# Attention scores by two heads and transposes by block, with projection matmuls between the pieces

## The chip, the cores and the metric

One core of one Trainium2 chip runs the whole program. The metric is the device time of one execution in microseconds (us), lower is better. Engines are called PE (matrix multiplication), DVE (vector), ACT (activation functions and copies), POOL (general) and SP (which issues most transfers).

## The reference

A two-layer encoder over two requests that share weights, 512 and 256 tokens of width 1024, all in 32-bit floats. Each layer is a half SwiGLU block, a mixer, and another half SwiGLU block; a final RMSNorm ends it. The first layer's mixer, the only part that the change touches, is this:

```python
def mixer_ab(h, w_in, sgu_ln_g, sgu_ln_b, sgu_w, sgu_b, sink, w_out):
    z = h @ w_in
    zs = gelu(z[..., :1024])
    u, vh = zs[..., :512], layer_norm(zs[..., 512:], sgu_ln_g, sgu_ln_b)
    vh = vh.reshape(B, L // 128, 128, 4, 128)
    vmix = einsum('gij,bnjgc->bnigc', sgu_w, vh) + sgu_b
    a_out = u * vmix                                      # gating half
    q, k, v = the other columns of z: 8 q heads, 2 k heads, 2 v heads of 64
    b_out = window_gqa(rope_partial(q), rope_partial(k), v, sink)
    return concatenate([a_out, b_out], axis=-1) @ w_out
```

`window_gqa` works on blocks of 128 queries. Each block sees the keys of its own block and of its two neighbours within 128 positions, four q heads share one k and v head, and one learned number per head (`sink`) joins the softmax as an extra column without a value.

## The kernel before, in words

Activations are kept transposed, features on the 128 partitions and tokens along the free axis, so 768 columns in all. A matmul of 32-bit floats is made of three products of rounded parts: each operand is split in a high part (ACT copies it to a rounded type) and a low part (DVE subtracts the high part from the original), and PE computes high times high, high times low and low times high into one PSUM bank. `mm3` issues these three, called a triple here. Weights arrive by transfer as `raw` and are split into `whi` (ACT) and `wlo` (DVE).

PE executes in the order in which the code is written. The order of the other engines' instructions is set by a scheduler from its own model. The written order is woven from a main line and side chains. The main line of the first mixer projects the q heads (`q_heads`, m = 0 to 3), the gating input (`vh_part`, called for three token blocks at a time: three PSUM tiles of 512 columns), the gate (`u_part`), and then the output (`mixer_out`). A side chain is a Python generator. It issues some work and yields a number, the microseconds of modelled PE work that must be issued before it goes on. After every triple `mm3` calls `tick()`, which resumes the chains whose number is due. `drain` runs a chain to its end at once, without triples between.

Three kinds of side chain matter here. `attention(GAP0)` walks over 12 steps, kv = 0, 1 and n = 0 to 5. A step has three parts. `score` issues the score matmuls of four q heads in two pairs m = 0, 1 (`scores2`, six matmuls a pair), and then the softmax in `finish_rows`: a DVE reduce for each head that adds the mask and finds the maximum, a negation, an ACT exponential for each head with its sum, the sink's exponential, a sum, a reciprocal and a DVE multiply for each head. `turn` transposes the probabilities, four PE transposes for each of two or three key blocks into one PSUM bank, and splits each bank into `th` (ACT) and `tl` (DVE). `values` multiplies with the values, copies half of the bank with ACT (`tb`) and adds the halves with four DVE instructions (`o`). The values of a step come after the scores of the next. The chains `sgu` (one for each of six token blocks) normalise a block of the gating input (`vg`), split it (`vhh`, `vhl`), mix it on PE with `mixed` (12 small matmuls) and scale and shift it from PSUM with four DVE instructions, also named `o`, at L1319. The third kind, `v_tokens`, prepares the values early.

PSUM has eight banks. The pool `mm` has four, used in turn by the projections, and `aux` has four, used in turn by scores, transposes, values and gating. A bank is taken again only when the engine that reads it has done so. The q heads' projections are read by `roped` on DVE: a shuffle (`ru`), two multiplications (`rt`, `ru`) and an add.

At the start of the output projection, `mixer_out` begins two output tiles with the inputs whose split is `e` (`eh`, `el`), and then goes on with inputs whose split is made there (`oh`, `ol`), by `parts`:

```python
            with self.tc.high_priority(), self.tc.issue_after(self.exps[-1]):
                parts(rest, 0)
```

`self.exps` is a list to which `finish_rows` appends its last exponential each time it is called, so that these splits come on ACT after the latest one written so far. What remains of the attention chain is drained near the end of that function.

Of the kernel before, what the change touches and what calls it, by code (L numbers as in the profile page):

```python
# [9 lines left out]
F32 = mybir.dt.float32  # L10
# [6 lines left out]
P = 128  # L17
# [29 lines left out]

WTOTAL = 12 * D * FF + 16 * EARLY * P * D + D * 1792 + 2 * D * D + D * 3072 + D * 512
VTOK = (4.0,9.0)
GAP0 = 5.2  # L50
SGU = (8.0, 3.0, 4.0)
NP, NQ = 16, 2
GAPS1 = (3.5, 0.6, 3.5, 0.8)
# [2 lines left out]
class Trunk:  # L56
# [1061 lines left out]
    def mixer0(self):  # L1118
        nc = self.nc
        mp = self.mixer_open("m0")  # L1120
# [8 lines left out]
        msk = mp.tile([P, 3 * P], F32, tag="msk", name="msk")  # L1129
        nc.sync.dma_start(msk, self.aps["gmask"])  # L1130
        sink = mp.tile([P, P], F32, tag="sink", name="sink")[:, :8]
# [18 lines left out]
        def roped(ps, c0, c1):  # L1150
            n = c1 - c0
            t, u = tmp("rt")[:, :n], tmp("ru")[:, :n]
            nc.vector.stream_shuffle(out=u, in_=ps[:, :n], mask=swap)
            nc.vector.tensor_tensor(out=t, in0=ps[:, :n], in1=rct[:, c0:c1], op=ALU.mult)
            nc.vector.tensor_tensor(out=u, in0=u, in1=rst[:, c0:c1], op=ALU.mult)
            nc.vector.tensor_tensor(out=t, in0=t, in1=u, op=ALU.add)
            return t
# [18 lines left out]
        for g in (0, 1):  # L1176
            c0, c1 = GROUPS[g]
            t = roped(pkv[g][0], c0, c1)
# [17 lines left out]
                self.q_split(*qs[g], t)  # L1196
            qheads.append(qs)

        def score(kv, qs, n):
            lo_b, hi_b = (0, 4) if n < 4 else (4, 6)  # L1200
            blks = list(range(max(n - 1, lo_b), min(n + 2, hi_b)))
            nk = len(blks)
            cols = slice(blks[0] * P, (blks[-1] + 1) * P)
            ps_list, ps = [], None
            for m in (0, 1):
                if nk == 3 or m == 0:
                    ps = [self.psum(self.aux, "aux") for _ in (0, 1)]
                o = 0 if nk == 3 else m * nk * P
                dst = [t[:, o : o + nk * P] for t in ps]
                q = [t[:, n % 4 * P : (n % 4 + 1) * P] for t in qs[m][n // 4]]  # L1210
                self.scores2(dst, q, (kh[kv][:, cols], kl[kv][:, cols]))
                ps_list += dst
            p = [mp.tile([P, 3 * P], F32, tag="p", name="p", bufs=4) for _ in range(4)]
            m0 = (blks[0] - n + 1) * P
            add = msk[:, m0 : m0 + nk * P]
            outs = [p[r][:, : nk * P] for r in range(4)]
            self.finish_rows(
                mp, 4, ps_list, outs, [add] * 4,
                [sink[:, 4 * kv + r : 4 * kv + r + 1] for r in range(4)], sink[:, 4 * kv : 4 * kv + 4],
            )  # L1220
            return kv, n, blks, p

        def turn(kv, n, blks, p):
            res = []
            for i, b in enumerate(blks):
                pt = self.psum(self.aux, "aux")
                for r in range(4):
                    self.tpose(pt[:, r * P : (r + 1) * P], p[r][:, i * P : (i + 1) * P])
                th = mp.tile([P, 512], F32R, tag="th", name="th", bufs=3)
                tl = mp.tile([P, 512], F32R, tag="tl", name="tl", bufs=3)  # L1230
                self.split(th, tl, pt)
                res.append((th, tl))
            return res

        def values(kv, n, blks, tt):
            po = self.psum(self.aux, "aux")
# [15 lines left out]
        qheads, scored, gates = [], [], []  # L1252
# [3 lines left out]
        def attention(gap):  # L1256
            cur = None
            for kv in (0, 1):
                for n in range(6):
                    while len(qheads) < 2 * kv + 2:  # L1260
                        yield 0.5
                    new = score(kv, qheads[2 * kv : 2 * kv + 2], n)
                    scored.append((kv, n))
                    yield gap
                    if cur:
                        values(*cur[:3], tt)
                        valued.append(cur[:2])
                    yield gap
                    cur = new
                    tt = turn(*cur)  # L1270
                    yield 0.3 * gap
            yield 1.0
            values(*cur[:3], tt)

# [10 lines left out]
        def offsets():  # L1285

            b = vhl()
            self.split(*b, lnb)
            yield VTOK[0]
            ps = self.psum(self.aux, "aux")  # L1290
            mixed(ps, b)
            nc.vector.tensor_tensor(out=sb, in0=ps, in1=sb, op=ALU.add)
# [65 lines left out]

        self.spawn(offsets())
        att = self.spawn(attention(GAP0))  # L1360
        for m in range(2):
            q_heads(m)
# [457 lines left out]
```

## Time and profile before

| | us |
|---|---|
| median of 3 runs | 2595.67 |
| lowest and highest | 2592.29, 2597.21 |
| profiled execution | 2597.41 |
| its span in the profile | 2595.6 |
| PE busy | 2556.4 (98%) |
| DVE busy | 2232.9 (86%) |
| ACT busy | 1365.6 (53%) |
| POOL busy | 159.7 (6%) |
| mean granted clock of PE | 0.994 of full speed |

The span is the time from the first to the last instruction in the profile; 1.8 us of the execution lie around it. An engine's busy time is the sum of its instructions. The granted clock is what a throttle leaves of PE's full speed: 0.5 means that matmuls take twice as long. The first mixer takes about 545 to 745 us of the span. Line numbers such as L1248 are those of the kernel before; in the changed kernel they are shifted by one or two.

### The profile page before, as it was taken

What the parts mean: (1) busy time and instruction counts of PE and PEld (TensorE: products, weight loads), DVE (VectorE), ACT (ScalarE), POOL (GpSimd) and SP (SyncE); (2) the same over time, 40 slices, a digit from 0 to 9 for tenths busy, and PEclk for the clock granted to TensorE, in tenths of its full rate; (3) what the DMA queues carried; (4) which work ended last, traced back from release to release, by engine and by line L of the source; (5) the groups of instructions that cost most, each with busy time, mean ns of one, the idle gap of its engine ahead of it and who ended that gap; (6) DMA issues with size and microseconds to landing.
All of it is one profiled execution on the core that took longest, in us unless ns stands there. A gap on an engine that the chain in (4) does not pass through costs nothing.

```text
span 2595.6 us, 41312 instructions
## 1 busy us (share of the span) xinstructions
PE 2556.4 (98%) x15114; PEld 2491.2 (96%) x15114; DVE 2232.9 (86%) x4659; ACT 1365.6 (53%) x2869; POOL 159.7 (6%) x255
## 2 busy tenths in 40 slices
PE   8999999999999999999999999999999999999998
PEld 8899999988899999999999999998998999999997
DVE  7898889888789998889998888986676699888897
ACT  7454454556656544445655445454454565444543
POOL 1000000000022000000100000002222220000000
PEclk9999999999999999999999999999999999999999
DMA  7523222321135322223442222142221344222222
GB/s 253 160 84 111 66 74 74 130 93 45 49 111 165 103 66 66 77 70 98 125 120 74 73 66 82 66 142 66 64 64 41 106 130 123 82 71 77 70 68 75
DMA packets 93372, 238.68 MB, mean 92 GB/s; under 512 B 21488, under 2 KB 34288, under 8 KB 93168
## 3 DMA queue, kind: packets, MB, share of 16 engines
q1 hardware_dynamic: 85712, 218.96, 26.5%
q0 software_dynamic: 7168, 16.78, 3.0%
q8 instruction: 119, 1.95, 0.3%
q14 instruction: 85, 0.70, 0.1%
q10 hardware_dynamic: 288, 0.29, 0.0%
HBM read 226.56 MB, written 15.07 MB: 93 GB/s over the span
## 4 chain that ended last, share of the span: by engine, by line
PE 68%; DVE 4%; ACT 1%; issue 1%; DMA 0%; DVEq 0%; ACTq 0%
PE ps_mm L152 41%; PE ps_aux L152 25%; PE ps_aux L156 1%; DVE wlo L123 0%; DVE tmp L415 0%; ACT p L1103 0%; DVE p L1113 0%; DVE p L1097 0%; DMA raw<-in_w 0%; ACT whi L122 0%; DVE tl L209 0%; DVE qk L1577 0%; DVE sg L589 0%; ACT diag L306 0%; DVE v L588 0%
## 5 line engine op out<-in xcount | busy, mean ns | idle before, releaser
L122 ACT CAST whi<-s 128x512 fp32r<-128x512 f32 x496 | 304.6, 620 | 404.5 <-DVE s L737 179.2
L122 ACT CAST whi<-raw 128x512 fp32r<-128x512 f32 x504 | 306.1, 619 | 224.3 <-PE ps_mm L152 95.3
L123 DVE TENSOR_TENSOR wlo<-s,whi 128x512 fp32r<-128x512 f32 x496 | 336.6, 684 | 59.9 <-ACT whi L122 50.4
L123 DVE TENSOR_TENSOR wlo<-raw,whi 128x512 fp32r<-128x512 f32 x468 | 319.9, 692 | 17.4 <-ACT whi L122 14.2
L152 PE MATMUL ps_aux<-dt,whi 128*128 128x384 f32 x864 | 221.8, 337 | 5.1 <-ACT whi L122 5.1
L152 PE MATMUL ps_mm<-db,whi 128*128 128x384 f32 x864 | 219.3, 334 | 0.0
L152 PEld LDWEIGHTS ps_aux<-dt,whi 128*128 128x128 f32 x864 | 157.7, 190 | 5.8 <-ACT whi L122 5.8
L152 PEld LDWEIGHTS ps_mm<-db,whi 128*128 128x128 f32 x864 | 156.0, 188 | 0.0
L152 PE MATMUL ps_aux<-dt,wlo 128*128 128x384 f32 x432 | 145.7, 337 | 0.2 <-DVE wlo L123 0.2
L152 PE MATMUL ps_mm<-xh,whi 128*128 128x512 f32 (+1 forms) x416 | 145.7, 350 | 0.0
L152 PE MATMUL ps_mm<-db,wlo 128*128 128x384 f32 x432 | 144.3, 334 | 0.0
L152 PE MATMUL ps_mm<-xh,wlo 128*128 128x512 f32 (+1 forms) x416 | 140.8, 338 | 0.0
L152 PE MATMUL ps_mm<-xl,whi 128*128 128x512 f32 (+1 forms) x416 | 140.8, 338 | 0.0
L737 DVE TENSOR_TENSOR s<-raw,raw 128x512 f32<-128x512 f32 x124 | 83.9, 685 | 25.1 <-DMA raw<-in_w 25.0
L577 DVE TENSOR_TENSOR u<-ps_aux,u 128x384 f32<-128x384 f32 x176 | 96.9, 551 | 7.6 <-PE ps_aux L152 7.4
L793 DVE TENSOR_TENSOR x<-ps_aux,x 128x384 f32<-128x384 f32 x160 | 85.3, 551 | 15.6 <-PE ps_aux L152 15.6
L152 PE MATMUL ps_aux<-dh,whi 128*128 128x384 f32 x384 | 97.5, 334 | 0.0
L123 POOL TENSOR_TENSOR wlo<-raw,whi 128x512 fp32r<-128x512 f32 x36 | 48.5, 1355 | 746.0 <-ACT whi L122 738.1
L1103 ACT ACTIVATE p<-p,st 128x256 f32<-128x256 f32 (+3 forms) x144 | 69.0, 480 | 47.9 <-DVE st L1101 47.8
L793 DVE TENSOR_TENSOR x<-ps_mm,x 128x384 f32<-128x384 f32 x160 | 85.8, 550 | 5.8 <-PE ps_mm L152 5.5
L572 ACT COPY u<-ps_mm 128x384 f32<-128x384 f32 x176 | 83.4, 474 | 10.7 <-PE ps_mm L152 10.4
L152 PEld LDWEIGHTS ps_mm<-xh,whi 128*128 128x128 f32 x416 | 79.2, 190 | 9.1 <-issue 0.8
(516 smaller groups left out, 8143.1 us busy)
## 6 DMA issues: line engine op xcount, KB each, us to landing
raw<-in_w SPq DMA_DIRECT2D x346, 512.0 KB, 3.7
s<-in_w POOLq DMA_DIRECT2D x64, 256.0 KB, 4.9
xdm<-x SPq DMA_DIRECT2D x16, 384.0 KB, 2.4
x<-in_x SPq DMA_DIRECT2D x16, 192.0 KB, 5.4
tok<-in_xt SPq DMA_DIRECT2D x12, 256.0 KB, 6.9
xold<-xdm SPq DMA_DIRECT2D x8, 384.0 KB, 3.1
x<-xdm SPq DMA_DIRECT2D x8, 384.0 KB, 4.5
out_y<-y SPq DMA_DIRECT2D x8, 384.0 KB, 2.6
```

Source lines behind the costliest of these rows:

```text
L122: nc.scalar.copy(hi, src)
L123: (eng or nc.gpsimd).tensor_tensor(out=lo, in0=src, in1=hi.bitcast(F32), op=ALU.subtract)
L152: self.nc.tensor.matmul(out, lhsT=lhsT, rhs=rhs, start=start, stop=stop, **kw)
L156: self.nc.tensor.transpose(out, src, self.ident)
L572: nc.scalar.copy(e[n, out], bank[key, n])
L577: nc.vector.tensor_tensor(out=t, in0=bank[key, n], in1=t, op=ALU.add)
L737: f = lambda o, x, y, op: self.nc.vector.tensor_tensor(out=o, in0=x, in1=y, op=op)
L793: nc.vector.tensor_tensor(out=o, in0=ps, in1=o, op=ALU.add)
L1103: ins = nc.scalar.activation(outs[i], outs[i], AF.Exp, bias=nm[:, i : i + 1], accum_out=sm[:, i : i + 1])
```

## The change

`score` becomes a generator that works on two heads at a time. Each pair takes two PSUM banks of its own (before, steps with two key blocks put both pairs into the same two banks), runs its six score matmuls, calls `finish_rows` for its two heads, and yields 1.5. `turn` becomes a generator that yields 0.8 after each block's four transposes. `attention` waits 3.4 (before 5.2) between the parts, and the pause of 0.3 times the gap after `turn` goes.

```diff
@@ -47,7 +47,8 @@
 
 WTOTAL = 12 * D * FF + 16 * EARLY * P * D + D * 1792 + 2 * D * D + D * 3072 + D * 512
 VTOK = (4.0,9.0)
-GAP0 = 5.2
+GAP0 = 3.4
+FINE = 1.5, 0.8
 SGU = (8.0, 3.0, 4.0)
 NP, NQ = 16, 2
 GAPS1 = (3.5, 0.6, 3.5, 0.8)
@@ -1196,32 +1197,29 @@
                 self.q_split(*qs[g], t)
             qheads.append(qs)
 
-        def score(kv, qs, n):
+        def score(kv, qs, n, res):
             lo_b, hi_b = (0, 4) if n < 4 else (4, 6)
             blks = list(range(max(n - 1, lo_b), min(n + 2, hi_b)))
             nk = len(blks)
             cols = slice(blks[0] * P, (blks[-1] + 1) * P)
-            ps_list, ps = [], None
+            m0 = (blks[0] - n + 1) * P
+            add = msk[:, m0 : m0 + nk * P]
+            p = []
             for m in (0, 1):
-                if nk == 3 or m == 0:
-                    ps = [self.psum(self.aux, "aux") for _ in (0, 1)]
-                o = 0 if nk == 3 else m * nk * P
-                dst = [t[:, o : o + nk * P] for t in ps]
+                dst = [self.psum(self.aux, "aux")[:, : nk * P] for _ in (0, 1)]
                 q = [t[:, n % 4 * P : (n % 4 + 1) * P] for t in qs[m][n // 4]]
                 self.scores2(dst, q, (kh[kv][:, cols], kl[kv][:, cols]))
-                ps_list += dst
-            p = [mp.tile([P, 3 * P], F32, tag="p", name="p", bufs=4) for _ in range(4)]
-            m0 = (blks[0] - n + 1) * P
-            add = msk[:, m0 : m0 + nk * P]
-            outs = [p[r][:, : nk * P] for r in range(4)]
-            self.finish_rows(
-                mp, 4, ps_list, outs, [add] * 4,
-                [sink[:, 4 * kv + r : 4 * kv + r + 1] for r in range(4)], sink[:, 4 * kv : 4 * kv + 4],
-            )
-            return kv, n, blks, p
-
-        def turn(kv, n, blks, p):
-            res = []
+                two = [mp.tile([P, 3 * P], F32, tag="p", name="p", bufs=4) for _ in range(2)]
+                heads = slice(4 * kv + 2 * m, 4 * kv + 2 * m + 2)
+                self.finish_rows(
+                    mp, 2, dst, [t[:, : nk * P] for t in two], [add] * 2,
+                    [sink[:, 4 * kv + 2 * m + r : 4 * kv + 2 * m + r + 1] for r in range(2)], sink[:, heads],
+                )
+                p += two
+                yield FINE[0]
+            res.append((kv, n, blks, p))
+
+        def turn(res, kv, n, blks, p):
             for i, b in enumerate(blks):
                 pt = self.psum(self.aux, "aux")
                 for r in range(4):
@@ -1230,7 +1228,7 @@
                 tl = mp.tile([P, 512], F32R, tag="tl", name="tl", bufs=3)
                 self.split(th, tl, pt)
                 res.append((th, tl))
-            return res
+                yield FINE[1]
 
         def values(kv, n, blks, tt):
             po = self.psum(self.aux, "aux")
@@ -1259,16 +1257,16 @@
                 for n in range(6):
                     while len(qheads) < 2 * kv + 2:
                         yield 0.5
-                    new = score(kv, qheads[2 * kv : 2 * kv + 2], n)
+                    new = []
+                    yield from score(kv, qheads[2 * kv : 2 * kv + 2], n, new)
                     scored.append((kv, n))
                     yield gap
                     if cur:
                         values(*cur[:3], tt)
                         valued.append(cur[:2])
                     yield gap
-                    cur = new
-                    tt = turn(*cur)
-                    yield 0.3 * gap
+                    cur, tt = new[0], []
+                    yield from turn(tt, *cur)
             yield 1.0
             values(*cur[:3], tt)
```

In the rows below, a row is one instruction with its line, its kind, what it writes and reads, and the shape; "x4" stands for so many alike in a row, and a number behind a name tells one tile from another.

The first place is PE at the third q heads' projection (`ps_mm_6380` and `ps_mm_6456`, 512 and 256 columns). Before, transposes of one step (kv 0, n 1) and scores of the next come as blocks:

```order
L152 MATMUL ps_mm_6380<-xh_5309,wlo_6373 128x512
L156 MATMUL ps_aux_6419<-ident,p 128x128 x4
L156 MATMUL ps_aux_6428<-ident,p 128x128 x4
L156 MATMUL ps_aux_6437<-ident,p 128x128 x4
L152 MATMUL ps_mm_6456<-xh_5302,whi_6372 128x256
L152 MATMUL ps_mm_6456<-xl_5310,whi_6372 128x256
L152 MATMUL ps_mm_6456<-xh_5302,wlo_6373 128x256
L152 MATMUL ps_aux_6460<-kh_5716,q_6008 128x384
L152 MATMUL ps_aux_6461<-kh_5716,q_6008 128x384
```

The changed kernel there (the same projection is `ps_mm_6394` and `ps_mm_6461`):

```order
L157 MATMUL ps_aux_6430<-ident,p 128x128 x4
L153 MATMUL ps_mm_6394<-xh_5309,whi_6390 128x512
L153 MATMUL ps_mm_6394<-xl_5317,whi_6390 128x512
L153 MATMUL ps_mm_6394<-xh_5309,wlo_6391 128x512
L157 MATMUL ps_aux_6442<-ident,p 128x128 x4
L153 MATMUL ps_mm_6461<-xh_5302,whi_6386 128x256
L153 MATMUL ps_mm_6461<-xl_5310,whi_6386 128x256
L153 MATMUL ps_mm_6461<-xh_5302,wlo_6387 128x256
L153 MATMUL ps_mm_6461<-xh_5303,whi_6386 128x256
L153 MATMUL ps_mm_6461<-xl_5311,whi_6386 128x256
L153 MATMUL ps_mm_6461<-xh_5303,wlo_6387 128x256
L157 MATMUL ps_aux_6468<-ident,p 128x128 x4
```

One or two triples now stand between blocks of four transposes, and the second score piece of the step moves to the end of this projection, right ahead of the next one's start, `vh_part(3)`:

```order
L153 MATMUL ps_aux_6516<-kh_5716,q_6094 128x384
L153 MATMUL ps_mm_6461<-xh_5308,whi_6390 128x256
L153 MATMUL ps_mm_6461<-xl_5316,whi_6390 128x256
L153 MATMUL ps_mm_6461<-xh_5308,wlo_6391 128x256
L153 MATMUL ps_mm_6461<-xh_5309,whi_6390 128x256
L153 MATMUL ps_mm_6461<-xl_5317,whi_6390 128x256
L153 MATMUL ps_mm_6461<-xh_5309,wlo_6391 128x256
L153 MATMUL ps_mm_6557<-whi_6562,xh_5302 128x512
L153 MATMUL ps_mm_6557<-wlo_6563,xh_5302 128x512
```

Those scores (`ps_aux_6516` is the last of them) are now followed on PE by two triples of 256 columns and then by the three tiles of `vh_part(3)` (`ps_mm_6557`, 6558, 6559).

DVE at the same place, before (6380 is the PSUM tile of the third q heads):

```order
L1097 ISA p,st<-ps_aux_6469,msk,sink 128x384
L1097 ISA st 128x1
L209 TENSOR_TENSOR vhl<-vg,vhh 128x512
L1101 TENSOR_SCALAR st<-st 128x4
L209 TENSOR_TENSOR vhl<-vg,vhh 128x512
L1107 TENSOR_TENSOR st<-sink,st 128x4
L123 TENSOR_TENSOR wlo_6609<-raw_6602,whi_6608 128x512
L1248 TENSOR_TENSOR o_5934<-ps_aux_6384,tb 64x128 x2
L1248 TENSOR_TENSOR o_5935<-ps_aux_6384,tb 64x128 x2
L1153 STREAM_SHUFFLE ru<-ps_mm_6380 128x512
L1154 TENSOR_TENSOR rt<-ps_mm_6380,rct 128x512
```

And DVE in the changed kernel (the same tile is 6394):

```order
L1098 ISA p,st<-ps_aux_6515,msk,sink 128x384
L1108 TENSOR_TENSOR st<-sink,st 128x2
L1246 TENSOR_TENSOR o_5934<-ps_aux_6407,tb 64x128 x2
L1246 TENSOR_TENSOR o_5935<-ps_aux_6407,tb 64x128 x2
L1098 ISA p,st<-ps_aux_6516,msk,sink 128x384
L1098 ISA st 128x1
L1154 STREAM_SHUFFLE ru<-ps_mm_6394 128x512
L1102 TENSOR_SCALAR st<-st 128x2
L210 TENSOR_TENSOR vhl<-vg,vhh 128x512
L1156 TENSOR_TENSOR ru<-ru,rst 128x512
L1155 TENSOR_TENSOR rt<-ps_mm_6394,rct 128x512
```

The last read of the tile, `rt`, still comes behind the scores' reduces, but those belong to matmuls that now stand later on PE, and one `vhl` and `ru` have moved ahead of it.

The second place is ACT at the start of the output projection (`oh_7589` and its like are the splits made by `parts`), before:

```order
L1103 ACT_TABLE_LOAD
L1103 ACTIVATE p,st<-p,st 128x384 x4
L1108 ACTIVATE st<-st 128x4
L208 CAST oh_7589<-o_5930 128x384
L208 CAST oh_7590<-o_5931 128x384
L208 CAST oh_7591<-o_5932 128x384
```

The changed kernel there:

```order
L1349 ACTIVATE ug<-ug 128x256
L1104 ACT_TABLE_LOAD
L1104 ACTIVATE p,st<-p,st 128x384 x2
L1109 ACTIVATE st<-st 128x2
L1104 ACTIVATE p,st<-p,st 128x384 x2
L1109 ACTIVATE st<-st 128x2
L209 CAST oh_7618<-o_5930 128x384
L209 CAST oh_7619<-o_5931 128x384
```

The exponentials ahead of the casts are of the same step (kv 1, n 2) but come in pairs, each with its sink's, and a gate tile (`ug`) has moved ahead of them. On PE the last score piece whose exponentials stand there (`ps_aux_7658`) now comes two triples ahead of the first that reads `oh`; before, some 50 rows lay between. The changed kernel's PE:

```order
L153 MATMUL ps_aux_7658<-kh_5717,q_6962 128x384
L153 MATMUL ps_mm_7679<-eh_5938,whi_7638 128x384
L153 MATMUL ps_mm_7679<-el_5940,whi_7638 128x384
L153 MATMUL ps_mm_7679<-eh_5938,wlo_7639 128x384
L153 MATMUL ps_mm_7679<-eh_5939,whi_7638 128x384
L153 MATMUL ps_mm_7679<-el_5941,whi_7638 128x384
L153 MATMUL ps_mm_7679<-eh_5939,wlo_7639 128x384
L153 MATMUL ps_mm_7650<-oh_7618,whi_7642 128x384
```

## The prediction

> **What bounds the kernel now.** First the totals of the page and its chain of waits, to see which engine sets the end.
>
> ```profile
> span 2595.6 us, 41312 instructions
> PE 2556.4 (98%) x15114; PEld 2491.2 (96%) x15114; DVE 2232.9 (86%) x4659; ACT 1365.6 (53%) x2869; POOL 159.7 (6%) x255
> PE 68%; DVE 4%; ACT 1%; issue 1%; DMA 0%; DVEq 0%; ACTq 0%
> ```
>
> PE is busy 98% of the span and is most of the chain. The matmuls are the same before and after, so the change can only give or take PE's idle time and the clock at which PE runs, and only in the first mixer, 545 to 745 us. Next the table of stretches there (columns: us, then busy time with count for PE, PE's weight loads, DVE, ACT and POOL, then the granted clock, DMA share and GB/s).
>
> ```profile
> 570.00:597.00 27.00, 24.25 (x136) 20.01 (x135) 23.69 (x78) 20.50 (x43) 0.00 (x0) 1.00 0.14 40
> 597.00:607.00 10.00, 9.48 (x49) 7.87 (x50) 8.39 (x26) 1.84 (x4) 0.00 (x0) 0.66 0.16 52
> 632.00:642.00 10.00, 8.54 (x45) 6.76 (x44) 9.93 (x32) 3.89 (x11) 0.00 (x0) 0.83 0.09 26
> 660.00:700.00 40.00, 37.98 (x231) 32.53 (x229) 33.34 (x85) 31.29 (x67) 4.66 (x3) 1.00 0.10 31
> 700.00:710.00 10.00, 8.10 (x41) 7.43 (x41) 7.45 (x18) 1.90 (x4) 1.29 (x1) 0.83 0.40 137
> sum 215.00, PE 206.13 PEld 181.28 DVE 172.66 ACT 124.62 POOL 16.43; mean PE 22.90 PEld 20.14 DVE 19.18 ACT 13.85 POOL 1.83
> ```
>
> The sum is over nine stretches, 545 to 760, of which these five lose most: PE idles 215 − 206.13 = 8.9 us. The clock column costs more: three stretches of 10 us at 0.66, 0.83 and 0.83, that is 10 × (0.34 + 0.17 + 0.17) = 6.8 us. So 15.7 us, 0.6% of the time, is the most that the change can gain. Who PE waited for is in its waits from 545 to 745 (idle us, count, longest).
>
> ```profile
> PE ps_aux L152 <- DVE tl L209: 3.4, 5, 1.5
> PE ps_mm L152 <- DVE wlo L123: 1.9, 1, 1.9
> PE ps_aux L156 <- DVE o L1319: 1.7, 1, 1.7
> PE ps_mm L152 <- DVE ol L209: 0.8, 1, 0.8
> ```
>
> All of these are waits for DVE: a backlog, not latency alone. In the timeline the longest three stand at the start of, or inside, the three stretches with the lower clock (start us, duration, engine, in brackets the wait before):
>
> ```profile
> 596.94 0.66 PE L156 MATMUL ps_aux<-ident,p 128*128 128x128 f32 x4 [1.66 <-DVE o L1319]
> 635.48 0.33 PE L152 MATMUL ps_aux<-swh,vhh 128*128 128x128 f32 x1 [1.46 <-DVE tl L209]
> 705.45 0.44 PE L152 MATMUL ps_mm<-oh,wlo 128*128 128x384 f32 x1 [1.90 <-DVE wlo L123]
> ```
>
> **The change, part by part.** Durations come from the groups by line and shape from 545 to 745 (busy us, mean ns).
>
> ```profile
> L1097 DVE CUSTOM_DVE_ANT_0 p<-ps_aux,msk,sink 128x384 f32<-128x384 f32 x16 | 9.0, 612 | 0.2 <-PE ps_aux L152 0.2
> L209 DVE TENSOR_TENSOR tl<-ps_aux,th 128x512 fp32r<-128x512 f32 x28 | 18.1, 683 | 6.2 <-ACT th L208 6.1
> L209 DVE TENSOR_TENSOR vhl<-vg,vhh 128x512 fp32r<-128x512 f32 x6 | 4.0, 688 | 1.8 <-ACT vhh L208 1.8
> L1248 DVE TENSOR_TENSOR o<-ps_aux,tb 64x128 f32<-64x128 f32 x48 | 16.2, 337 | 1.9 <-ACT tb L1242 1.3
> L1153 DVE STREAM_SHUFFLE ru<-ps_mm 128x512 f32<-128x512 f32 x3 | 2.2, 743 | 0.1
> L1154 DVE TENSOR_TENSOR rt<-ps_mm,rct 128x512 f32<-128x512 f32 x3 | 2.0, 674 | 0.0
> L1155 DVE TENSOR_TENSOR ru<-ru,rst 128x512 f32<-128x512 f32 x3 | 2.0, 682 | 0.0
> L1101 DVE TENSOR_SCALAR st<-st 128x4 f32<-128x4 f32 x12 | 2.0, 163 | 0.1
> L209 DVE TENSOR_TENSOR ol<-o,oh 128x384 fp32r<-128x384 f32 x16 | 8.3, 551 | 0.1
> L1103 ACT ACTIVATE p<-p,st 128x384 f32<-128x384 f32 x16 | 9.7, 604 | 3.9 <-DVE st L1101 3.9
> L1103 ACT ACT_TABLE_LOAD x7 | 9.0, 1283 | 0.1
> L208 ACT CAST th<-ps_aux 128x512 fp32r<-128x512 f32 x28 | 15.0, 589 | 19.3 <-PE ps_aux L156 19.2
> L208 ACT CAST oh<-o 128x384 fp32r<-128x384 f32 x16 | 7.4, 519 | 3.4 <-DVE o L1248 3.4
> L1108 ACT ACTIVATE st<-st 128x4 f32<-128x4 f32 x12 | 2.3, 188 | 0.0
> ```
>
> And what a projection triple (three matmuls) takes, from the first and the ninth matmul in a row of 512 columns in the timeline (start us, duration, the rest): 1.83 us for eight, 0.229 each, so 0.69 for a triple of 512, 0.52 for 384, 0.34 for 256.
>
> ```profile
> 545.03 0.39 PE L152 MATMUL ps_mm<-xh,whi 128*128 128x512 f32 x1
> 546.86 0.39 PE L152 MATMUL ps_mm<-xh,wlo 128*128 128x512 f32 x1
> ```
>
> *Removed.* Scores no longer come in twelves, nor transposes in eights and twelves, so the waits above lose their place: I count all 8.9 us as gone and price what stands in the new order as new waits. That includes the 1.9 us for wlo: in the new DVE order the subtraction of that weight stands ahead of the probability multiplies.
>
> *Added.* Four small DVE instructions (maximum negated, sink add, sum add, reciprocal) now run twice for each of 12 steps: 48 × 0.163 = 7.8 us, and 12 more exponentials of 0.188 on ACT, which two fewer table loads pay. DVE is free for 42 us of the 215, so the 7.8 us are hidden except where it is full (9.93 of 10 in the stretch from 632); if that cover went everywhere they would cost 7.8. I put them at 0 and let the waits below carry them. POOL's and SP's orders do not change, so no DMA is issued elsewhere.
>
> *New wait 1, start of the second gating projection.* Three 512-column tiles take new banks of the four in the pool mm. The third must wait until DVE has read the rotary product of the third q heads. After the second score piece, PE has two triples of 256 and two of 512: 2.1 us. On DVE ahead of that read now stand a reduce, a sink add, four o, the other reduce, the shuffle, a negation, a vhl, ru and rt: 0.61 + 0.16 + 1.35 + 0.61 + 0.74 + 0.16 + 0.69 + 0.68 + 0.67 = 5.7 us. Wait 5.7 − 2.1 = 3.6. Lower end 2.0, if the first reduce, the o and the adds run while PE still scores (1.35 + 0.16 off); upper end 5.5, if the transposes just ahead also queue for the gating groups' DVE work as they did for 1.7. I take 3.5, nearest the plain sum. Before, that read came here, and no wait for it is in PE's list:
>
> ```profile
> 589.32 0.67 DVE L1154 TENSOR_TENSOR rt<-ps_mm,rct 128x512 f32<-128x512 f32 x1
> ```
>
> *New wait 2, start of the output projection.* Its first o splits are issued only after the last exponential that has been issued by then (the list `exps`). Before, this was the sink exponential of a step whose scores lay well ahead:
>
> ```profile
> 682.99 0.19 ACT L1108 ACTIVATE st<-st 128x4 f32<-128x4 f32 x1
> 683.08 1.32 ACT L208 CAST oh<-o 128x384 fp32r<-128x384 f32 x3
> 687.46 0.33 PE L152 MATMUL ps_mm<-oh,whi 128*128 128x384 f32 x1
> ```
>
> The cast was done over 3 us before PE came to it. Now the last exponential belongs to a score piece that stands two e triples, 1.03 us, ahead of the first o triple on PE. Behind it come two reduces, a negation, two exponentials, the sink's, an oh and an ol: 1.22 + 0.16 + 1.21 + 0.19 + 0.52 + 0.55 = 3.85, less 1.03: lower end 2.8. Upper end 6.2: ACT must also do a table load and the first pair's exponentials first, 1.28 + 1.21 + 0.19, and another 0.7 is one DVE instruction such as tl in front. I take 5.0, above the middle, because DVE has ol, o, wlo and the multiplies of the first pair waiting there, and is busy 33.34 of 40 us in that stretch.
>
> *New wait 3, second group of the gating mix.* A score piece waits for a tl that stands behind two vhl, shuffle, rt and ru: 1.38 + 0.74 + 1.36 = 3.5, and 4.2 with the final rotary add, which no row above shows apart and which I estimate at rt's 0.67. PE has some 2.5 us there (seven 256 triples 2.4). I take 1.6; ends 0 and 5.3 (4.2 with another 1.1 of gating work ahead).
>
> *New wait 4, the end of attention.* Eight transposes and four value matmuls come without a triple between: th 0.59 and tl 0.68, 1.27 in all, little of it covered. 1.2, ends 0 and 1.5.
>
> *What stays of the old waits* where DVE is full: 1.0, ends 0 (the pieces are spread enough) and 3.5 (the tl waits just as now).
>
> *Clock.* New waits 1, 2 and 3 are as long as those with which the three half-clock stretches began, so I expect about three again: 0, ends −5.1 (only one short stretch stays, 6.8 − 1.7) and +3.4 (two more of 1.7).
>
> [...]
>
> *Sum.* −8.9 + 3.5 + 5.0 + 1.6 + 1.2 + 1.0 + 0 = +3.4 us. The profiled execution took 2597.41, 1.74 above the median of 2595.67; so 2600.8 in its frame, 2599.1 in the median's.
>
> **The rivals.** *Slower, by the output projection.* New wait 2 comes to its upper end, 6.2, since nothing can pass the last exponential on ACT, wait 1 to 4.5, and each pulls one more half-clock stretch of 1.7: −8.9 + 4.5 + 6.2 + 3.8 + 3.4 = +9.0, 2604.7. It decides where wait 2 passes 5.1 with those two stretches left in place: −8.9 + 4.5 + 5.1 + 3.8 = 4.5, and any clock loss then takes it over 5.2. For it: DVE's load and an ACT queue in order. Against it: ACT is only 58% busy here (124.62 of 215), so the first pair may be done early.
>
> *Faster, the pieces do their work.* Waits 1 and 2 at their lower ends (2.0, 2.8), 0.8 for wait 3, 0.9 for the rest, and all but one short half-clock stretch gone: −8.9 + 6.5 − 5.1 = −7.5, 2588.2. For it: every wait of before was one for DVE behind a burst, and DVE has 42 us free. Against it: the two dependences of waits 1 and 2 are fixed by the order, whatever the pieces.
>
> *The transposes themselves pull the clock down*, and blocks of four with a triple between no longer do. Then the three stretches go and the waits stay as forecast: +3.4 − 6.8 = −3.4, 2592.3. Against it: this row, twelve in a row at full clock (the stretch from 660 has 1.00).
>
> ```profile
> 689.02 1.47 PE L156 MATMUL ps_aux<-ident,p 128*128 128x128 f32 x12
> ```
>
> [...]
>
> **How the numbers follow.** 0.2%, 5.2 us, is about what a measurement of this kernel can tell from no change: faster is under 2590.5, slower over 2600.9. The forecast has 0.43, of which 0.07 lies over 2600.9 (its own range is 2594 to 2603); the slower rival 0.25; the faster one 0.25; the transposes' 0.07, of which 0.02 under 2590.5. So faster 0.27, same 0.41, slower 0.32. The range goes from 2588, which leaves out half of the faster rival (0.12), to 2607, which leaves out a third of the slower one (0.08).
>
> **What would show it.** In the waits of the changed kernel: a ps_mm wait for DVE rt of 2 to 5 us at the start of the second gating projection (about 588 us); a ps_mm wait for oh or ol of 3 to 6 us at the first o triple (about 685 us); wlo gone from the list. In the stretches: three at less than full clock. Wrong it would be if both waits are under 2 us, because DVE or ACT takes the pieces in another order of time than I read, or if the clock stays at 1.00 after waits of 3 us, or if half speed follows each piece.

## The result and the profile after

The changed kernel took 2600.73 us (median of 13 runs, 2598.01 to 2607.46), the kernel before on the same chips 2594.58 (13 runs, 2591.77 to 2598.29). The ratio is 1.0025, with a 95% interval from 1.0018 to 1.0032: slower by about 6 us. The profiled execution took 2600.43, with a span of 2598.7.

The totals of the changed kernel's page:

```profile
span 2598.7 us, 41352 instructions
PE 2557.5 (98%) x15114; PEld 2487.8 (96%) x15114; DVE 2237.6 (86%) x4707; ACT 1365.8 (53%) x2879; POOL 158.5 (6%) x255
```

PE has the same 15,114 matmuls, and DVE the 48 more instructions. PE's waits in the first mixer, 540 to 760 us (idle us, count, longest), stand against the list of before:

```profile
PE ps_mm L153 <- ACT oh L209: 4.2, 1, 4.2
PE ps_mm L153 <- DVE rt L1155: 3.0, 1, 3.0
PE ps_aux L153 <- DVE tl L210: 2.3, 3, 1.1
PE ps_aux L153 <- ACT th L209: 0.9, 1, 0.9
PE ps_mm L153 <- DVE ol L210: 0.6, 1, 0.6
PE ps_aux L153 <- DVE vhl L210: 0.2, 1, 0.2
```

Of the waits of before, those for wlo and both o are gone, and tl has shrunk. (The second wait for an o, the smaller one, was this row in the kernel before.)

```profile
PE ps_aux L152 <- DVE o L1248: 0.5, 1, 0.5
```

In their place stand one for oh, at the first o triple, and one for rt, at the third tile of `vh_part(3)`. In the timeline:

```profile
584.40 0.39 PE L153 MATMUL ps_mm<-xh,whi 128*128 128x256 f32 x1
589.00 0.69 DVE L1155 TENSOR_TENSOR rt<-ps_mm,rct 128x512 f32<-128x512 f32 x1
589.74 0.50 PE L153 MATMUL ps_mm<-whi,xh 128*128 128x512 f32 x1 [2.97 <-DVE rt L1155]
633.87 0.33 PE L153 MATMUL ps_aux<-swh,vhh 128*128 128x128 f32 x1 [0.58 <-DVE tl L210]
686.18 2.15 ACT L209 CAST oh<-o 128x384 fp32r<-128x384 f32 x5
686.73 0.45 PE L153 MATMUL ps_mm<-oh,whi 128*128 128x384 f32 x1 [4.19 <-ACT oh L209]
737.73 1.58 DVE L1246 TENSOR_TENSOR o<-ps_aux,tb 64x128 f32<-64x128 f32 x4
738.88 0.49 PE L153 MATMUL ps_aux<-th,vt 128*128 128x512 f32 x1 [0.86 <-ACT th L209]
740.51 0.50 PE L153 MATMUL ps_aux<-tl,vt 128*128 128x512 f32 x1 [1.13 <-DVE tl L210]
```

Stretches of the changed kernel, 545 to 765 us (busy us and count of PE, PE's weight loads, DVE, ACT, POOL, then PE's granted clock, DMA share, GB/s), and the same sum of the kernel before behind them:

```profile
545.00:600.00 55.00, 51.42 (x284) 41.89 (x283) 46.19 (x147) 32.11 (x69) 0.00 (x0) 0.97 0.19 59
600.00:645.00 45.00, 44.19 (x261) 36.00 (x261) 37.89 (x135) 27.76 (x63) 0.00 (x0) 1.00 0.17 58
645.00:685.00 40.00, 37.53 (x231) 31.33 (x230) 34.65 (x101) 29.43 (x64) 3.87 (x3) 1.00 0.16 47
685.00:700.00 15.00, 12.64 (x66) 11.94 (x66) 10.26 (x26) 5.68 (x15) 0.93 (x1) 0.89 0.08 26
700.00:730.00 30.00, 30.00 (x186) 27.21 (x185) 23.01 (x70) 12.56 (x34) 4.27 (x4) 1.00 0.31 97
730.00:765.00 35.00, 33.01 (x181) 31.78 (x178) 24.69 (x63) 16.61 (x37) 6.39 (x5) 0.95 0.33 110
sum 220.00, PE 208.79 PEld 180.14 DVE 176.68 ACT 124.16 POOL 15.46; mean PE 34.80 PEld 30.02 DVE 29.45 ACT 20.69 POOL 2.58
```

```profile
sum 220.00, PE 211.13 PEld 186.28 DVE 177.66 ACT 128.27 POOL 16.43; mean PE 35.19 PEld 31.05 DVE 29.61 ACT 21.38 POOL 2.74
```

Idle is 220 − 208.79 = 11.2 us against 8.9. Three stretches have less than full clock, each behind one of the new waits (3.0, 4.2 and, at the end, 0.9 and 1.1 us): 55 × 0.03 + 15 × 0.11 + 35 × 0.05 = 5.1 us lost against 6.8. Together that is +0.6 us. But the mixer as a whole is 4.1 us longer in these two profiles, as one matmul ahead of it and one behind it show, first in the kernel before, then the same two in the changed kernel:

```profile
510.69 0.33 PE L152 MATMUL ps_aux<-dh,wlo 128*128 128x384 f32 x1
...
866.73 0.33 PE L152 MATMUL ps_aux<-b222h,wlo 128*128 128x384 f32 x1
```

```profile
509.79 0.34 PE L153 MATMUL ps_aux<-dh,wlo 128*128 128x384 f32 x1
...
869.92 0.34 PE L153 MATMUL ps_aux<-b222h,wlo 128*128 128x384 f32 x1
```

It runs 0.9 us ahead at 510 us and 3.2 behind at 870. The missing 3.5 us lie inside what the profile calls busy (3.9 us, when idle and clock are taken between these same two matmuls, as in the table under "Whole score blocks"). A step's scores before, twelve matmuls of 256 columns in one block:

```profile
648.14 0.28 PE L152 MATMUL ps_mm<-xh,wlo 128*128 128x256 f32 x1
648.35 0.39 PE L152 MATMUL ps_aux<-kh,q 64*128 64x256 f32 x2
...
649.25 0.39 PE L152 MATMUL ps_mm<-xh,whi 128*128 128x256 f32 x1
649.48 0.28 PE L152 MATMUL ps_mm<-xl,whi 128*128 128x256 f32 x1
```

and the first of the two pieces of six in the changed kernel:

```profile
649.93 0.40 PE L153 MATMUL ps_mm<-xh,wlo 128*128 128x512 f32 x1
650.26 0.39 PE L153 MATMUL ps_aux<-kh,q 64*128 64x256 f32 x2
...
650.81 0.50 PE L153 MATMUL ps_mm<-xh,whi 128*128 128x512 f32 x1
651.15 0.40 PE L153 MATMUL ps_mm<-xl,whi 128*128 128x512 f32 x1
```

From the start of the last projection matmul to the start of the second one behind the scores, less the two pitches that these two would take (0.12 for 256 columns, 0.229 for 512): 1.34 − 0.24 = 1.10 us for twelve together, and 1.22 − 0.46 = 0.76 for six alone. A piece pays some 0.1 us each where PE turns to score matmuls (0.33 us from start to start, where the pitch is 0.229), on the first pair of them (0.22 where 0.12), where it turns back (0.21 where 0.12), and on the first projection matmul after that (0.34 where 0.229). Over all undisturbed blocks the medians are 1.11 (5 blocks) and 0.76 (15 blocks) for 256 columns, 1.45 (one block; the other three hold waits) and 0.92 (8) for 384. So cutting costs 2 × 0.76 − 1.11 = 0.41 us in the eight steps with 256 columns and 2 × 0.92 − 1.45 = 0.39 in the four with 384: 4.8 us. A block of four transposes takes 0.44 us (25 blocks), of eight 0.88 (7), of twelve 1.32 (3), by the same count: three blocks of four take what the one of twelve takes, so cutting those cost PE nothing here.

### The profile page after: what moved, and what is told of

It is laid out like the page before. It is cut to its first block, busy times and chain, and to the rows that moved or that the text cites. A ratio compares the mean times of both kernels' runs of the same rounds, so it can differ in the third digit from the quotient of the medians.

```text
span 2598.7 us, 41352 instructions
## 1 busy us (share of the span) xinstructions
PE 2557.5 (98%) x15114; PEld 2487.8 (96%) x15114; DVE 2237.6 (86%) x4707; ACT 1365.8 (53%) x2879; POOL 158.5 (6%) x255
## 4 chain that ended last, share of the span: by engine, by line
PE 89%; DVE 6%; ACT 2%; DMA 2%; issue 1%; SPq 0%; DVEq 0%; ACTq 0%
PE ps_mm L153 54%; PE ps_aux L153 34%; PE ps_aux L157 1%; DMA raw<-in_w 1%; DVE wlo L124 1%; ACT p L1104 1%; DVE p L1098 0%; DVE tmp L416 0%; DMA x<-in_x 0%; ACT whi L123 0%; DVE s L738 0%; DVE tl L210 0%; DMA first<-in_w 0%; DVE p L1114 0%; DVE o L1246 0%
## 5 line engine op out<-in xcount | busy, mean ns | idle before, releaser
L153 PE MATMUL ps_mm<-oh,whi 128*128 128x384 f32 x252 | 88.4, 351 | 4.2 <-ACT oh L209 4.2
```

The costliest lines, as they stand in the source:

```text
L153: self.nc.tensor.matmul(out, lhsT=lhsT, rhs=rhs, start=start, stop=stop, **kw)
```

## The experiments

Theory A is the prediction's: the change replaces waits by waits at a few fixed places. Rival B: the finer pieces cost by their small instructions, wherever they stand. Theory C came after the first nine runs: cutting the scores costs PE time in itself.

| kernel | median us | ratio to before, 95% interval |
|---|---|---|
| changed kernel | 2600.73 | 1.0025 [1.0018, 1.0032] |
| o splits after an earlier exponential | 2594.26 | 0.9998 [0.9989, 1.0007] |
| third gating tile later | 2598.0 | 1.0013 [1.0004, 1.0022] |
| both of these | 2590.84 | 0.9985 [0.9976, 0.9994] |
| both, and gap 3.0 in the second half | 2588.2 | 0.9975 [0.9966, 0.9985] |
| changed kernel with gap 3.2 | 2597.63 | 1.0012 [1.0003, 1.0021] |
| before, scores alone cut | 2607.75 | 1.0050 [1.0036, 1.0064] |
| before, transposes alone cut | 2608.47 | 1.0052 [1.0040, 1.0065] |
| before, gap 3.4 alone | 2614.54 | 1.0085 [1.0072, 1.0099] |
| before, softmax by two heads | 2592.15 | 0.9990 [0.9981, 0.9999] |
| the repaired kernel with whole score blocks | 2589.09 | 0.9982 [0.9973, 0.9991] |
| the same, third tile still later | 2587.46 | 0.9974 [0.9965, 0.9984] |

**The wait for oh.**

```diff
-            with self.tc.high_priority(), self.tc.issue_after(self.exps[-1]):
+            with self.tc.high_priority(), self.tc.issue_after(self.exps[-3]):
                 parts(rest, 0)
```

> The changed kernel, but the first o splits of the output projection are issued after the last exponential of the step before (third from the end of the list) instead of the last one. Theory A (the change replaces waits by waits at a few fixed places, each with a half-clock stretch behind it): PE's wait for oh of 4.2 us and the one for ol of 0.6 us fall to under 1 us together, the half-clock stretch at 687 us goes with them (1.7 us), all else stays: 4 to 6.5 us less than the changed kernel, ratio to the kernel before 1.0000 to 1.0010. Rival B (the finer pieces cost in themselves, by 48 more small DVE instructions and more handoffs spread over the mixer): the wait goes but comes back elsewhere in the mixer, no more than 2 us less, ratio 1.0017 to 1.0025.

The ratio is 0.9998, 6 to 7 us off the changed kernel: just past the end of what A expected, and far from what B did. PE's list there, 540 to 760 us, has lost oh, ol and the 0.2 us for vhl, and kept the rest:

```profile
PE ps_mm L153 <- DVE rt L1155: 3.0, 1, 3.0
PE ps_aux L153 <- DVE tl L210: 2.3, 3, 1.1
PE ps_aux L153 <- ACT th L209: 1.0, 1, 1.0
```

This one dependence of new wait 2, with what follows it, is as large as the whole loss of the change.

**The wait for rt.**

```diff
-                for i in range(3):
-                    a, b = (n0 + i) * P, (n0 + i + 1) * P
-                    st = (self.xh[k][:, a:b], self.xl[k][:, a:b])
-                    self.mm3(ps[i], st, w[k % 2], k == 0, k == KD - 1)
+                late = n0 and k < 2
+                todo = [(k, i) for i in range(2 if late else 3)]
+                if late and k:
+                    todo += [(0, 2), (1, 2)]
+                for j, i in todo:
+                    a, b = (n0 + i) * P, (n0 + i + 1) * P
+                    st = (self.xh[j][:, a:b], self.xl[j][:, a:b])
+                    self.mm3(ps[i], st, w[j % 2], j == 0, j == KD - 1)
```

> The changed kernel, but vh_part(3) issues the first two weights' triples of its first two tiles before any of its third tile, so that the third tile's bank is wanted two triples (1.37 us) later. Theory A: PE's wait for rt of 3.0 us falls by just that, to 1.6 us, and the time by 1.4 us (3.1 if the half-clock stretch behind it goes too): ratio to the kernel before 1.0012 to 1.0020. Rival B: the wait is only a sign of a full DVE, and what is saved there is waited for at the next gating or score matmuls: ratio as the changed kernel's, 1.0025, within 0.0004.

The ratio, 1.0013, is where A had it, but not by A's steps. The wait went altogether, since a gating mix and the values of a step stand between the triples, so that the third tile came later than 1.37 us; and of what was saved, 1.5 us came back at that mix, as the rival said it would:

```profile
594.61 0.30 PE L153 MATMUL ps_aux<-swh,vhh 128*128 128x128 f32 x1 [1.02 <-DVE o L1317]
595.50 0.33 PE L153 MATMUL ps_aux<-swh,vhl 128*128 128x128 f32 x1 [0.48 <-DVE vhl L210]
```

**Both repairs.** The two edits together.

> The changed kernel with both repairs: the first o splits issued after the last exponential of the step before, and vh_part(3) with its third tile later. Theory A (waits at separate places on one chain of PE): the two gains add up, 6.5 and 2.7 us: some 2591.5 us, ratio to the kernel before 0.9980 to 0.9996, and no oh and no rt wait in PE's list. Rival (PE gains earlier but DVE is the bound behind it): the second repair gives less than 1 us beside the first, ratio 0.9994 to 1.0002.

0.9985: the gains add up (0.9998 and 1.0013 against 1.0025 would give 0.9986), and neither oh nor rt is in PE's list.

**The drain.** Beside both repairs, in `attention`:

```diff
             for kv in (0, 1):
+                if kv:
+                    gap = 3.0
                 for n in range(6):
```

> As the kernel with both repairs, and with the gap 3.0 instead of 3.4 in the second half of the attention (kv 1) only, so that the last step's transposes and values come on PE with projection triples between and nothing is drained back to back. Theory A: the last waits for th and tl (1.0 and 1.1 us) and the half-clock stretch behind them (1.7) go too, 2 to 3.8 us less than with both repairs: ratio to the kernel before 0.9968 to 0.9986. Rival: the shifted pieces meet a new wait, as the gap of 3.2 did at the gating mix: no less than with both repairs, ratio 0.9985 to 1.0000.

0.9975, as A expected, though the intervals of this and of both repairs overlap. PE's whole list from 545 to 765 us and its sum there:

```profile
PE ps_aux L153 <- DVE tl L210: 1.5, 3, 0.6
PE ps_aux L153 <- DVE o L1319: 1.0, 1, 1.0
PE ps_aux L153 <- DVE vhl L210: 0.7, 2, 0.5
```

```profile
sum 220.00, PE 216.69 PEld 189.24 DVE 188.33 ACT 136.19 POOL 21.37; mean PE 36.12 PEld 31.54 DVE 31.39 ACT 22.70 POOL 3.56
```

3.3 us idle, and the clock is 1.00 in every stretch. A kernel with the pieces can thus be faster than the kernel before, by 0.25%, once the three places are mended. What the same repairs would give in the kernel before was not run, so the gain is not shown to come from the pieces.

**The places shifted.**

```diff
-GAP0 = 3.4
+GAP0 = 3.2
```

> The changed kernel with the gap between the parts of a step 3.2 instead of 3.4. The pieces stay as fine, but their places on PE shift: the score piece ahead of the output projection now has ten triples behind it before the first o triple, and the attention ends by itself instead of being drained; the start of vh_part(3) stays as it is. Theory A: the rt wait of 3.0 us stays, the waits for oh, ol and those at the drain (th, tl: 2.0 us) fall to under 1.5 us together, two half-clock stretches go: 6 to 9 us less than the changed kernel, ratio to the kernel before 0.9988 to 1.0002. Rival B: the time depends on the pieces, not on where they fall: ratio 1.0017 to 1.0030.

A's number missed: 1.0012. The waits for oh, ol and at the drain went, the one for rt stayed at 3.0, as expected; but the second gating group had moved too, and there a new wait had come that A had not looked for, and the clock lost 6.9 us where the changed kernel lost 5.1:

```profile
646.28 0.48 PE L153 MATMUL ps_aux<-swh,vhl 128*128 128x128 f32 x1 [3.75 <-DVE vhl L210]
```

That a gap of 0.2 us trades one wait of 4 us for another says that places decide, and that one has to look at all of them.

**Parts of the change alone.** Scores cut, all else as before:

```diff
-                    new = score(kv, qheads[2 * kv : 2 * kv + 2], n)
+                    new = []
+                    yield from score(kv, qheads[2 * kv : 2 * kv + 2], n, new)
...
-                    cur = new
+                    cur = new[0]
                     tt = turn(*cur)
                     yield 0.3 * gap
```

(`score` itself as in the change.)

> The kernel before with the scores alone cut in two pieces of two heads (a pause of 1.5 after each); transposes whole, gaps 5.2 and the pause of 0.3 gap as before. Because the two pauses make a step longer, the attention falls behind and its last four steps are drained without triples between. Theory A: each place where score or transposes come back to back at the end costs waits of 3 to 5 us: slower than the kernel before by 10 to 25 us, ratio 1.004 to 1.010, all of it in the drain at the end of the output projection and not in the first 100 us of the mixer. Rival B: the cost is in the pieces: half of the change's 6 us, spread over the mixer, ratio 1.001 to 1.002.

Transposes cut, all else as before:

```diff
-                    cur = new
-                    tt = turn(*cur)
+                    cur, tt = new, []
+                    yield from turn(tt, *cur)
                     yield 0.3 * gap
```

> The kernel before with the transposes alone cut by blocks (a pause of 0.8 after each block), scores whole, gaps 5.2 and the pause of 0.3 gap as before. The step is longer, so the last step and a half are drained without triples. Theory A: 4 to 6 us of waits in that drain, where scores, transposes and values stand back to back, 1 to 3 us of the old waits gone earlier: ratio 1.0005 to 1.0020, and up to 700 us not later than the kernel before. Rival (the transposes' bursts pull the clock down): no half-clock stretch before the drain, ratio 0.9975 to 0.9995.

The gap alone shortened, in the kernel before:

```diff
-GAP0 = 5.2
+GAP0 = 3.4
```

> The kernel before with the gap 3.4 instead of 5.2 and nothing else: scores and transposes whole. The steps come in three quarters of the PE work and the attention ends before the output projection. Theory A (places and room decide): between the scores and the transposes that need their softmax stand only 6 to 7 us of PE work, where the softmax of four heads takes some 7 us (four reduces 2.4, four exponentials 2.4, four multiplies 1.6, small ones 0.8), so each step brings 0.5 to 1.5 us of waits for p: slower by 3 to 12 us, ratio 1.001 to 1.005, with waits for p and tl in PE's list in the first 140 us of the mixer and none in the output projection. Rival (the shorter gap is what repairs the change, and the pieces alone cost): no slower than the kernel before, ratio 0.998 to 1.0005.

All three were slower than the change as a whole. The first had its number, 1.0050, and by the same matmuls as above 12.1 us more in the mixer, of which some 10 come after about 725 us, in the drain. Low clock is a large part there, 35 × 0.24 = 8.4 us:

```profile
730.00:765.00 35.00, 30.70 (x141) 24.91 (x140) 27.59 (x84) 18.97 (x49) 3.65 (x3) 0.76 0.16 48
```

The second lost more than expected, 1.0052. In its waits the transposes of three steps wait for probabilities, two of them after 730 us and one, of 5.1 us, long before any drain, which A had not expected. There PE had left the step's scores at 622.9 us, but the gating mix that took one of their banks waited until 631.08 for DVE's reduce of it, and the transposes until 637.77 for the probabilities:

```profile
PE ps_aux L157 <- DVE p L1114: 12.0, 3, 5.1
```

```profile
622.87 0.50 PE L153 MATMUL ps_mm<-xh,whi 128*128 128x512 f32 x1
631.08 0.33 PE L153 MATMUL ps_aux<-swh,vhh 128*128 128x128 f32 x1 [0.96 <-DVE st L1098]
637.77 2.12 PE L157 MATMUL ps_aux<-ident,p 128*128 128x128 f32 x8 [5.14 <-DVE p L1114]
```

The third lost nearly twice the most that A had expected, 1.0085. Waits for p came as A said, though four of the nine after 685 us, and one for a q head on top:

```profile
PE ps_aux L156 <- DVE p L1113: 8.7, 9, 1.7
PE ps_aux L152 <- ACT q L1373: 4.4, 1, 4.4
```

So neither cut is a gain without a gap that fits, nor the shorter gap without the cuts.

**The small instructions.** The kernel before, with the softmax called for two and two heads behind the twelve score matmuls.

```diff
-            self.finish_rows(
-                mp, 4, ps_list, outs, [add] * 4,
...
+            for m in (0, 1):
+                self.finish_rows(
+                    mp, 2, ps_list[2 * m : 2 * m + 2], outs[2 * m : 2 * m + 2], [add] * 2,
...
```

> The kernel before, with PE's order untouched, but finish_rows called twice per step for two heads each: the small DVE and ACT instructions of the change (48 and 12 more) without its pieces. Theory A: they are hidden in DVE's idle time: ratio 0.9995 to 1.0008 (at most 2 us, where DVE is full around 600 and 635 us). Rival B: they are the price of the change: 48 times 0.163 us is 7.8 us on DVE, ratio 1.0015 to 1.0030.

0.9990: not a cost, if anything a gain, perhaps since the first two heads' softmax no longer waits for the others' reduces (that reason is not shown). This takes the price of 7.8 us out of the account, and B with it.

**Whole score blocks.** The repaired kernel (with the gap of 3.0), the twelve score matmuls together again, their softmax by two and two heads.

```diff
...
             for m in (0, 1):
-                dst = [self.psum(self.aux, "aux")[:, : nk * P] for _ in (0, 1)]
+                if nk == 3 or m == 0:
+                    ps = [self.psum(self.aux, "aux") for _ in (0, 1)]
+                o = 0 if nk == 3 else m * nk * P
+                dst = [t[:, o : o + nk * P] for t in ps]
...
                 self.scores2(dst, q, (kh[kv][:, cols], kl[kv][:, cols]))
+                parts.append(dst)
+            for m in (0, 1):
...
-                yield FINE[0]
+            yield 2 * FINE[0]
```

> The kernel with both repairs and the late gap of 3.0, but the 12 score matmuls of a step stand together on PE again (banks as in the kernel before), followed by the softmax of two and two heads and one pause of 3.0. Theory C (each extra entry into and exit from a block of score matmuls costs PE time that the profile counts as busy: 1.11 us for twelve of 256 columns between two triples, against two times 0.76 for two sixes; 0.4 us for each of 12 steps): 4 to 5 us less of PE time, given back in part where four heads at once meet a full DVE: ratio to the kernel before 0.9952 to 0.9972. Rival A (only the places and the waits count, cutting the scores costs PE nothing): the old waits behind twelve score matmuls come back, 2 to 6 us: ratio 0.9980 to 1.0000.

0.9982: inside the range of A and outside that of C. The rt wait came back with 2.5 us:

```profile
593.09 0.50 PE L153 MATMUL ps_mm<-whi,xh 128*128 128x512 f32 x1 [2.54 <-DVE rt L1155]
```

```profile
sum 220.00, PE 215.43 PEld 190.55 DVE 187.49 ACT 134.75 POOL 19.95; mean PE 35.91 PEld 31.76 DVE 31.25 ACT 22.46 POOL 3.33
```

This kernel idles 4.6 us and loses 3.5 to the clock (0.97 in the stretch from 545, 0.96 in that from 600), 4.8 more than the repaired kernel with cut scores. By the ratio it is only 0.0007 or 1.8 us slower, and the two intervals overlap. What the whole blocks gave back can be read more closely between the two matmuls used above, ahead of the mixer and behind it, with the same 2000 matmuls between them in each kernel:

| us between the same two matmuls | before | changed | repaired, scores cut | repaired, scores whole | the same, third tile still later |
|---|---|---|---|---|---|
| time | 356.0 | 360.1 | 347.2 | 347.9 | 345.8 |
| PE idle | 10.9 | 12.8 | 4.2 | 5.9 | 5.9 |
| lost in half-clock stretches | 6.8 | 5.1 | 0.0 | 3.4 | 0.0 |
| the rest: PE busy, at full clock | 338.3 | 342.2 | 343.0 | 338.6 | 339.9 |

The last row is what C is about. It is 342 to 343 us in the kernels with cut scores and 338 to 340 in those with whole ones, 4.4 us less in this run than with cut scores. So C's cost is there, and was given back; the ratio fell into A's range because 1.7 us of idle time and 3.4 of low clock came back, more than C had allowed for. The run makes the blocks whole and gives both pairs the same banks again at once; that the cost lies at the blocks' ends is read from their rows above.

**The third tile still later.** As the last, with four weights' triples held back instead of two.

```diff
...
-                late = n0 and k < 2
+                late = n0 and k < 4
...
-                if late and k:
-                    todo += [(0, 2), (1, 2)]
+                if late and k == 3:
+                    todo += [(j, 2) for j in range(4)]
```

> The kernel with whole score blocks, and vh_part(3) holds its third tile back by four weights' triples instead of two. Theory C with A: the rt wait of 2.5 us that came back with whole blocks goes, and the half-clock stretch behind it (1.7) with it, while the score blocks keep their 1.1 us: 3 to 4.5 us less, ratio to the kernel before 0.9958 to 0.9976. Rival (five buffers for the weights' splits, four of them held: PE waits for a split instead): ratio 0.9978 to 0.9995, with a wait for wlo or whi near 590 us.

0.9974, just inside what C with A expected. The rt wait and the low clock went, as expected, no wait for a weight's split came; but the gating mix behind it then waited 1.6 us for an o and 1.4 for vhl. It is level with the repaired kernel with cut scores, whose blocks cost more and which waits less. These two are the fastest versions here, both faster than the kernel before and the changed one.

## Why the prediction was right, and where it was not

*Removed, 8.9 us of idle.* The waits for wlo and for both o are gone, and the 1.9 us for wlo as the order of DVE said. Right in what was named.

*New wait 1, 3.5.* Measured 3.0, at the place and for the read that were named. From the end of the scores (584.4, where the next triple starts) to the end of rt (589.7) it was 5.3 us where the sum had 5.7, and PE had 2.4 of work in that time where the sum had 2.1. (The upper end given, 5.5, should be 5.3: 3.6 and 1.7.)

*New wait 2, 5.0.* Measured 4.2 for oh and 0.6 for ol: 4.8. The cast comes right behind the sink's exponential on ACT. A first part of the delay was a DVE instruction of 128 × 2 that took 1.20 us. A POOL subtraction ran over it. Of the changed kernel's 24 such instructions on that line, the 22 beside no POOL subtraction took 0.18 us at most, the two beside one 0.49 and 1.20:

```profile
681.04 1.29 POOL L124 TENSOR_TENSOR wlo<-raw,whi 128x512 fp32r<-128x512 f32 x1 [6.08 <-ACT whi L123]
681.15 1.20 DVE L1102 TENSOR_SCALAR st<-st 128x2 f32<-128x2 f32 x1
```

*New wait 3, 1.6.* Measured 0.6 for tl and 0.2 for vhl: under the middle, inside the ends. It was the gating mix that waited for the tl, not a score piece.

*New wait 4, 1.2.* Measured 0.9 and 1.1, 2.0 in all, and a half-clock stretch behind it. The upper end, 1.5, was too low: four o of the step before, 1.58 us, stood on DVE ahead of the tl.

*What stays, 1.0.* Measured 0.6. All waits together 11.2 against 12.3 forecast: idle +2.3 instead of +3.4.

*Clock, 0.* Three stretches again, as the forecast had, but all of them short, 3.41 us each: 5.1 us lost against 6.8, −1.7.

*The step that failed* is the first sentence on the change: "The matmuls are the same before and after, so the change can only give or take PE's idle time and the clock". The same matmuls took longer here in other company: a step's twelve score matmuls of 256 columns, with the turns to them and back, 2 × 0.76 us in two pieces and 1.11 in one. Twelve more entries into score blocks cost 4.8 us by the blocks' own times, which the sum had at nothing. With the idle time and the clock as measured and without this term, the sum is 2.3 − 1.7 = 0.6. With it, it is 0.6 + 4.8 = 5.4, against 4.1 between the two profiles and 6 between the medians. Counted by the distance from each matmul's start to the next, less what that shape takes undisturbed, the sum closes: of the 4.1 us, 4.8 lie at the score blocks, 1.1 at waits, −2.1 at half clock and 0.3 elsewhere. So the two long waits are where the forecast had them, but idle and clock together all but cancel, and the loss is 6 us and not under 1 by a term that the forecast left out. That the time came out so near the forecast is in part luck: the terms that it had too high (idle 1.1, clock 1.7) hid part of the one that it had at nothing. What the slower rival asked for, wait 2 at its upper end with more low clock, did not happen.

*The transposes as a cause of low clock,* the last rival, were not set apart from waits by any run here. The kernel before, with whole transposes, lost 6.8 us to the clock and the changed one, with cut transposes, 5.1, both behind waits (1.5 to 1.9 us in the one; 3.0, 4.2, and 0.9 with 1.1 in the other). The repaired kernel with cut transposes and the last one lost 0.0.

## What to carry to other kernels

Before cutting work into pieces between other matmuls, measure in the trace what one entry into and exit from such a block costs, from the pitch of the neighbours, and multiply by the pieces: busy time hides it. Then look for what fixed dependences the moved pieces land next to (a bank that is read late, an "issue after the latest" rule, a drain at the end of a chain), because each cost 2 to 5 us here; mending them gave 0.5%, the difference between a loss of 0.25% and a gain of 0.25%.

## What was not expected of the hardware

The switch itself: 64-row score matmuls run in pairs (two start 3 to 4 ns apart), and turning to them and back costs 0.4 us, the first pair and the first projection matmul after it included (why was not tried), while turning to transposes and back costs nothing beside the transposes themselves, 0.11 us each (0.44 us for four, 1.32 for twelve).

Longer waits do not always mean a lower clock. The stretch from 600 to 645 has a wait of 0.6 us for a tl in the changed kernel, with 0.2 for vhl besides, at 1.00 as shown. In the kernel with the earlier exponential it has the first of these alone, and a lower clock:

```profile
600.00:645.00 45.00, 44.36 (x258) 36.16 (x257) 37.87 (x136) 27.43 (x64) 0.00 (x0) 0.96 0.19 59
```

0.96 of 45 us is 1.8 us lost, about one more short stretch at half. In the changed kernel's mixer the clock is 0.50 in three stretches of 3.413 us, from 591.64, 687.21 and 741.83 us; these starts lie 28 and 16 times 3.413 us apart. What sets where a stretch begins, and so which waits are followed by one, no run here shows. One stretch costs 1.7 us by the clock, and 1.6 by the matmuls' pitch, since at 0.50 those of 512 columns start 0.427 us apart and at full clock 0.228 (medians of this profile), 1.9 times and not quite twice. The mean granted clock differs between executions of one program: the changed kernel's 13 runs have 0.992 to 0.996, which is some 10 us of their time, and the one with 0.992 is the longest, 2607.46. So a difference of one stretch between two single profiles need not come from the kernels.

The two small DVE instructions beside a POOL subtraction, 0.49 and 1.20 us where the other 22 took 0.18 at most, may be another source of such differences; whether they change from execution to execution was not measured.
